# Gate projections in blocks of 128 features, half of them placed between the key and query tiles

## The chip, the cores and the metric

The kernel runs on one core of one Trainium2 chip. The time is device microseconds of one execution; the figure before the change is the median of three executions, and one further execution was taken with the hardware profiler.

## What is computed

One layer of a backbone over 1024 latent tokens of width 1024 (and 256 context tokens). Each token is normed and modulated to `h`, and one matrix `w_in` projects it to all inputs of two branches:

```
z = modulate(x, p['norm1_w'], sh1, sc1) @ w_in
q, k = z[..., 0:1024], z[..., 1024:2048]        # each rms_norm over 64, then rotary
v, u = z[..., 2048:3072], z[..., 3072:3584]
g = z[..., 3584:]                               # 2048 gate features
...
y_attn = diff_head_out(blocked_latent_diff_attention(q, k_all, v_all, lam), ...)
y_s5, _ = s5_branch(u, uc, p, update_ctx)       # linear recurrence, both directions, then GELU and GLU
g_s, g_a = split(g + b_gate, 2)
x = x + ga1 * ((sigmoid(g_s) * y_s5 + sigmoid(g_a) * y_attn) @ w_out)
x = x + ga2 * conv_ffn(modulate(x, p['norm2_w'], sh2, sc2), ...)
```

The gates `g` depend on `h` and on their weights alone. They are read much later, when the branches are merged.

## The kernel before

The modulated tokens stay in SBUF as two tables, `hTh` and `hTl` (a rounded high part and a remainder), and every projection is three products for each of the eight slices of the inner dimension: high by high, high by low and low by high. A unit of 128 outputs by 512 is thus 24 matmuls of 512 columns.

`phase_a` (L318) makes the projections in this order: u; keys (slabs 0 and 1, ten token tiles each, the last two of them context); values (slabs 2 and 3, ten tiles each); queries (slabs 5 and 6, eight tiles each); gates (slabs 7 to 10, L544). A slab is 512 features. `load_slab` (L586) fetches it in four quarters of 512 KB on the SP queue; ScalarE casts each quarter to the high part (L594) and GpSimd subtracts for the low part (L595). There are three buffers for raw weights and five each for high and low parts. The projected tile lies in a PSUM buffer "z", of which there are five for all projections.

- **Keys and queries.** `qk_post` (L633) takes a tile of 128 tokens: ScalarE squares (L638), VectorE reduces (L640, L641), ScalarE takes a square root (L644), VectorE the reciprocal and a Newton step (L645 to L648) and the two rotary products (L652, L656), GpSimd adds and scales (L657, L663), ScalarE scales six of the eight heads of a key tile (L662), TensorE transposes (L667), ScalarE and VectorE take the result out of PSUM (L670, L671), and SP stores it.
- **Recurrence.** Its parameters (`s5_params`, L758, generator `params`) are computed piece by piece beside the key tiles, mostly on VectorE. Its inputs are made beside the value tiles. `s5_scan` (L925) runs 158 steps one after the other, four small VectorE instructions each (L934 to L937): ten steps after each of the last value tiles, six after each query tile, and the rest in one call before the gates.
- **adaLN.** `adas` is a generator of small matmuls with loads of their own (L299, L302), one piece after each query tile.
- **Gates.** Here the weights are the stationary operand. For each of 16 blocks of 128 features and each half of the tokens there is one unit: 24 matmuls (L554 to L556), a tanh on ScalarE into one of two "stage" buffers (L558), and a store issued on ScalarE's queue (L559).
- **After the recurrence.** `s5_out_quad` (L940), eight of them, one after every second gate unit, at high priority: copies of the states on VectorE (L955, L956), matmuls (L962, L964); after every second one `s5_transpose` (L1187) stores the result. Then `s5_tail` (L1269) as a generator, one piece after each later gate unit: load and GELU (L1278, L1279), split into parts on VectorE and GpSimd (L1257, L1258), eight GLU units with a tanh (L1288), then sixteen branch units of 12 matmuls that end in L1310. The last four of the sixteen run inside the attention.
- **Attention** (`phase_b`, L969) follows. Its pool takes the memory of the token tables, which the gates read. Then come the merge, the output projection and the feed-forward (`phase_c`, L1324).

The order on each engine is set by a scheduler when the kernel is built: it takes the instructions by their order in the program (earlier ones first, high priority ahead of all) as they become ready on its own model of time. On the chip each engine runs its list in that fixed order.

Of the kernel before, what the change touches and what calls it, by code (L numbers as in the profile page):

```python
# [10 lines left out]
F32R = mybir.dt.float32r  # L11
I32 = mybir.dt.int32
AF = mybir.ActivationFunctionType
OP = mybir.AluOpType
# [4 lines left out]
P = 128  # L19
D = 1024  # L20
KT = D // P
L = 1024
NT = L // P
# [14 lines left out]
QUADS = G // 4  # L38
# [18 lines left out]
def pack(x, c, ctx, c_ctx, ada_w, ada_b, norm1_w, w_in, b_gate, q_norm_w, k_norm_w,  # L57
# [6 lines left out]
    def put(name, a):  # L64
        A[name] = np.ascontiguousarray(a)
# [10 lines left out]
    def perm64(a):  # L76
# [3 lines left out]
    w = np.asarray(w_in)[0]  # L80
    wq, wk = perm64(w[:, :1024]), perm64(w[:, 1024:2048])
    slabs = [wk[:, :512], wk[:, 512:], w[:, 2048:2560], w[:, 2560:3072], w[:, 3072:3584],
             wq[:, :512], wq[:, 512:]] + [w[:, 3584 + 512 * j:4096 + 512 * j] for j in range(4)]
    put("win", np.stack([s.reshape(2, 4, P, 512).transpose(0, 2, 1, 3) for s in slabs]))
    put("rows", np.concatenate([perm64(np.asarray(q_norm_w)), perm64(np.asarray(k_norm_w)), np.asarray(lam_q1),
                                np.asarray(lam_k1), np.asarray(lam_q2), np.asarray(lam_k2)], 1))
# [22 lines left out]
    def wtiles(a):  # L109
        k, m = a.shape  # L110
        return a.reshape(k // P, P, m // P, P).transpose(2, 1, 0, 3)

    put("wglu", wtiles(np.asarray(glu_w)[0]))
    put("wbs", wtiles(np.asarray(w_branch_s5)[0]))
    put("wba", wtiles(np.asarray(w_branch_attn)[0]))
# [8 lines left out]
    n = (NT * np.arange(P)[:, None] + np.arange(NT)[None, :])  # L124
# [10 lines left out]
def r32(ap):  # L135
    return ap.bitcast(F32)


class Kern:
# [178 lines left out]
    def phase_a(self):  # L318
# [91 lines left out]
        def project(tt, W, pz=None, ks=range(KT)):  # L410
            pz = self.t(ps, [P, 512], "z", 5) if pz is None else pz
            A = (hTh, hTl) if tt < NT else (cTh, cTl)
            tok = slice(tt % NT * P, tt % NT * P + P)
            for k in ks:
                wh, wl = W[0][k // 2][:, k % 2], W[1][k // 2][:, k % 2]
                hh, hl = A[0][k][:, tok], A[1][k][:, tok]
                nc.tensor.matmul(pz, hh, wh, start=k == 0, stop=False)  # L417
                nc.tensor.matmul(pz, hh, wl, start=False, stop=False)  # L418
                nc.tensor.matmul(pz, hl, wh, start=False, stop=k == KT - 1)  # L419
            return pz  # L420

        W = ([], [])
# [81 lines left out]
                next(params, None)  # L504
        zp, zp_st = self.pool("pk")
        self.rope_tables(zp, "K")
        for s in (0, 1):
            W = self.load_slab(wp, s)
            for tt in range(NKT):
                self.qk_post(zp, ps, project(tt, W), "K", s, tt)  # L510
                if tt % 4 == 3:
                    next(params, None)
        zp_st.close()
# [19 lines left out]
        for s in (5, 6):  # L533
            W = self.load_slab(wp, s)
            for tt in range(NT):
                self.qk_post(zp, ps, project(tt, W), "Q", s - 5, tt)
                next(adas, None)
                self.s5_scan(xp, self.scan_at + 6)
        zp_st.close()
        self.s5_scan(xp, NCH + NCC)  # L540
        yp, yp_st = self.pool("s5y")
        nq = 0
        tail = None
        for s in range(7, 11):  # L544
            W = self.load_slab(wp, s)
            for mm in range(4):
                m = (s - 7) * 4 + mm
                for hf in range(2):
                    tok = slice(hf * 512, hf * 512 + 512)
                    pz = self.t(ps, [P, 512], "z", 5)  # L550
                    for k in range(KT):
                        wh = W[0][k // 2][:, k % 2, mm * P:mm * P + P]
                        wl = W[1][k // 2][:, k % 2, mm * P:mm * P + P]
                        nc.tensor.matmul(pz, wh, hTh[k][:, tok], start=k == 0, stop=False)  # L554
                        nc.tensor.matmul(pz, wh, hTl[k][:, tok], start=False, stop=False)
                        nc.tensor.matmul(pz, wl, hTh[k][:, tok], start=False, stop=k == KT - 1)  # L556
                    g = self.t(gp, [P, 512], "stage", 2)
                    nc.scalar.activation(g, pz, AF.Tanh, scale=0.5, bias=self.hbg[:, m:m + 1])  # L558
                    nc.scalar.dma_start(self.Gd[m][:, tok], g)  # L559
                    next(adas, None)  # L560
                    if hf and nq < QUADS:
                        if nq % 2 == 0:
                            Yq = self.t(yp, [P, NT, P], "Yq", 1)
                        with self.tc.high_priority():
                            self.s5_out_quad(yp, ps, nq, Yq, xp)
                            nq += 1
                            if nq % 2 == 0:
                                self.s5_transpose(yp, ps, Yq, nq // 2 - 1)
                        if nq == QUADS:
                            for _ in adas:  # L570
                                pass
                            ap_st.close()
                            yp_st.close()
                            xp_st.close()
                            tail = self.s5_tail(ps)
                    elif tail:
                        next(tail, None)
        gp_st.close()
        wp_st.close()
        hp_st.close()  # L580
# [1 line left out]
        self.attn_open()  # L582
        for _ in tail:
            pass

    def load_slab(self, wp, s, qs=(0, 1, 2, 3)):  # L586
        nc = self.nc
# [941 lines left out]
```

## Time and profile before

| | |
|---|---|
| median of three executions | 2129.47 us (2129.38 to 2130.86) |
| the profiled execution | 2130.76 us |
| its span, first to last instruction | 2129.0 us |
| TensorE busy, matmuls | 2049.0 us |
| VectorE busy | 1185.0 us |
| GpSimd busy | 815.3 us |
| ScalarE busy | 741.8 us |

A busy share is the mean over stages that are limited by different things, so it is to be read stage by stage: in which stretch TensorE has idle time, and which engine is full in that stretch. TensorE's granted clock is given as a share of 2.4 GHz; its lower level is half of that. A matmul's record lasts longer than the distance to the next one (matmuls are pipelined), so the work of TensorE is measured from start to start.

### The profile page before, as it was taken

Reading aid. Unit: us, or ns where it says so; the run is one execution under the profiler, and the core shown is the slowest. Engines: PE = TensorE matmul, PEld = TensorE weight load, DVE = VectorE, ACT = ScalarE, POOL = GpSimd, SP = SyncE. Lnnn points to the kernel's source line nnn. Section 1 sums busy time; section 2 is a strip of 40 time slices with the busy share of each in tenths; the row PEclk is TensorE's granted clock in tenths of the full one; section 3 lists DMA queues with packets and bytes.
Section 4 is the critical chain, followed back from the end, with each engine's and each line's share of the span. In section 5 each row is a group of like instructions: output and inputs, shape, how many; then the busy total and the mean of one; then the engine's idle time right before and its main releaser. Section 6 shows DMA issues by size and latency. Waiting matters only on the chain. (4 is left out here: it accounts for less than half of the span.)

```text
span 2129.0 us, 28497 instructions
## 1 busy us (share of the span) xinstructions
PE 2049.0 (96%) x10656; PEld 1684.4 (79%) x10656; DVE 1185.0 (56%) x2363; ACT 741.8 (35%) x1349; POOL 815.3 (38%) x923
## 2 busy tenths in 40 slices
PE   6988999998999999999999989999999999999998
PEld 4766778865677887999999878878888888888887
DVE  6998944899962224888888653443323323233233
ACT  4434424221223313788888611332112212112121
POOL 1467411243211630366666646433323323223221
PEclk9998999999999999999999999999999999999999
DMA  9345575345667237322321145111111111111102
GB/s 324 105 116 139 124 207 175 120 123 164 202 198 233 95 107 234 93 78 86 113 78 53 36 163 179 49 45 50 52 47 50 46 43 45 47 52 46 50 15 99
DMA packets 150506, 227.84 MB, mean 107 GB/s; under 512 B 27104, under 2 KB 85856, under 8 KB 150368
## 3 DMA queue, kind: packets, MB, share of 16 engines
q1 hardware_dynamic: 140288, 207.67, 32.2%
q10 hardware_dynamic: 10080, 18.35, 2.3%
q8 instruction: 84, 1.38, 0.3%
q14 instruction: 54, 0.44, 0.1%
HBM read 168.76 MB, written 57.21 MB: 106 GB/s over the span
## 5 line engine op out<-in xcount | busy, mean ns | idle before, releaser
L1266 PE MATMUL up<-act,whi 128*128 128x512 f32 x704 | 276.5, 393 | 2.3 <-POOL act L1419 2.1
L1265 PE MATMUL up<-act,whi 128*128 128x512 f32 x704 | 276.1, 392 | 0.0
L1267 PE MATMUL up<-act,wlo 128*128 128x512 f32 x704 | 275.0, 391 | 0.0
L1505 DVE SCALAR_TENSOR_TENSOR y<-up,small,y 128x896 f32<-128x896 f32 (+1 forms) x176 | 123.9, 746 | 237.7 <-ACT y L1500 235.9
L1253 POOL TENSOR_TENSOR wlo<-wraw,whi 128x1024 fp32r<-128x1024 f32 (+1 forms) x64 | 141.5, 2212 | 276.6 <-ACT whi L1252 240.7
L1240 DVE TENSOR_REDUCE mx<-sc 128x1 f32<-128x1280 f32 x128 | 190.7, 1491 | 53.7 <-PE sc L1239 52.8
L595 POOL TENSOR_TENSOR wlo<-wraw,whi 128x1024 fp32r<-128x1024 f32 x40 | 97.4, 2451 | 244.4 <-ACT whi L594 242.4
L417 PE MATMUL z<-whi,hTh 128*128 128x512 f32 x448 | 182.2, 411 | 3.6 <-ACT hTh L406 3.6
L418 PE MATMUL z<-wlo,hTh 128*128 128x512 f32 x448 | 181.0, 405 | 0.4 <-POOL wlo L595 0.3
L419 PE MATMUL z<-whi,hTl 128*128 128x512 f32 x448 | 180.0, 404 | 0.2 <-DVE hTl L408 0.2
L993 ACT ACTIVATE e<-sc,mx 128x1280 f32<-128x1280 f32 x128 | 171.7, 1342 | 10.5 <-DVE mx L1240 8.9
L1038 PE MATMUL ta<-V,at 128*128 128x128 f32 x1280 | 168.1, 275 | 0.7 <-ACT at L1027 0.7
L1482 DVE SCALAR_TENSOR_TENSOR x<-z,modT,x 128x512 f32<-128x512 f32 x72 | 53.6, 750 | 203.6 <-PE z L1267 203.6
L1252 ACT CAST whi<-wraw 128x1024 fp32r<-128x1024 f32 (+1 forms) x64 | 62.0, 969 | 294.3 <-PE up L1266 156.1
L1266 PEld LDWEIGHTS up<-act,whi 128*128 128x128 f32 x704 | 132.3, 188 | 32.2 <-POOL act L1419 3.4
L1038 PEld LDWEIGHTS ta<-V,at 128*128 128x128 f32 x1280 | 155.5, 191 | 1.0 <-ACT at L1027 0.9
L1265 PEld LDWEIGHTS up<-act,whi 128*128 128x128 f32 x704 | 132.2, 188 | 29.8 <-DVE act L1417 0.2
L1267 PEld LDWEIGHTS up<-act,wlo 128*128 128x128 f32 x704 | 132.2, 188 | 28.7
L1238 PE MATMUL sc<-K,q 128*128 128x512 f32 (+1 forms) x384 | 148.2, 386 | 2.2 <-ACT e L993 2.2
L1239 PE MATMUL sc<-K,q 128*128 128x512 f32 (+1 forms) x384 | 131.8, 357 | 0.0
L1253 POOL TENSOR_TENSOR wdlo<-wdraw,wdhi 128x512 fp32r<-128x512 f32 (+1 forms) x40 | 56.3, 1409 | 183.5 <-ACT wdhi L1252 183.3
L1266 PE MATMUL z<-gt,wdhi 128*128 128x512 f32 x320 | 124.6, 389 | 1.0 <-POOL gt L1258 1.0
(436 smaller groups left out, 4610.1 us busy)
## 6 DMA issues: line engine op xcount, KB each, us to landing
wraw<-in_win_dram SPq DMA_DIRECT2D x44, 512.0 KB
wraw<-in_wup_dram SPq DMA_DIRECT2D x44, 512.0 KB
araw<-in_ada_dram SPq DMA_DIRECT2D x32, 512.0 KB
q<-Qd SPq DMA_DIRECT2D x128, 128.0 KB
Kd<-st SPq DMA_DIRECT2D x80, 128.0 KB
K<-Kd SPq DMA_DIRECT2D x16, 640.0 KB
aw<-in_ada_dram SPq DMA_DIRECT2D x16, 512.0 KB
Qd<-st SPq DMA_DIRECT2D x32, 256.0 KB
```

Source lines behind the costliest of these rows:

```text
L417: nc.tensor.matmul(pz, hh, wh, start=k == 0, stop=False)
L418: nc.tensor.matmul(pz, hh, wl, start=False, stop=False)
L419: nc.tensor.matmul(pz, hl, wh, start=False, stop=k == KT - 1)
L993: nc.scalar.activation(em, S[i]["sc"][m][:, :LK], AF.Exp, bias=S[i]["mx"][:, m:m + 1], accum_out=S[i]["l1"] if m else S[i]["l0"])
L1038: nc.tensor.matmul(PO[p][:, j * P:j * P + P], AT[p, kt // 2][:, kt % 2, j * P:j * P + P], W[:, kt], start=kt == 0, stop=kt == NKT - 1)
L1238: nc.tensor.matmul(sc[:, a:b], Q[0][:, m, qs], K[m][:, a:b], start=True, stop=False)
L1239: nc.tensor.matmul(sc[:, a:b], Q[1][:, m, qs], K[m][:, a:b], start=False, stop=True)
L1240: nc.vector.tensor_reduce(S["mx"][:, m:m + 1], sc[:, :LK], axis=AX.X, op=OP.max, negate=True)
L1253: nc.gpsimd.tensor_tensor(l, raw, r32(h), op=OP.subtract)
L1265: mm(o, W[0][:, k], ah[k], start=k == 0, stop=False)
L1266: mm(o, W[0][:, k], al[k], start=False, stop=False)
L1267: mm(o, W[1][:, k], ah[k], start=False, stop=k == n - 1)
```

## The change

The gate weights are packed as 16 blocks of 1024 by 128 (`wg`) and not as four slabs of 512 features. A generator `gates` yields after each unit. Four units are drawn beside each key slab and four beside each query slab, so that 16 of the 32 units stand there; the other 16 follow the queries as before. In each query slab, four tiles now carry eight scan steps (four on either side of a gate unit) and the other four carry four steps, where every tile had six. Of the units after the queries each of the first eight is followed by a quad (before: every second unit), and each of the last eight by a piece of the tail.

```
-             wq[:, :512], wq[:, 512:]] + [w[:, 3584 + 512 * j:4096 + 512 * j] for j in range(4)]
+             wq[:, :512], wq[:, 512:]]
...
+    put("wg", wtiles(w[:, 3584:]))
...
+        gates = self.gates(wp, ps, hTh, hTl)
         for s in (0, 1):
             W = self.load_slab(wp, s)
             for tt in range(NKT):
                 self.qk_post(zp, ps, project(tt, W), "K", s, tt)
+                if tt in (1, 2, 5, 6):
+                    next(gates)
                 if tt % 4 == 3:
                     next(params, None)
...
                 self.qk_post(zp, ps, project(tt, W), "Q", s - 5, tt)
+                if tt in (1, 2, 4, 5):
+                    self.s5_scan(xp, self.scan_at + 4)
+                    next(gates)
                 next(adas, None)
-                self.s5_scan(xp, self.scan_at + 6)
+                self.s5_scan(xp, self.scan_at + 4)
...
-        for s in range(7, 11):
-            W = self.load_slab(wp, s)
-            for mm in range(4):
...
+        for _ in gates:
+            next(adas, None)
+            if nq < QUADS:
...
+                with self.tc.high_priority():
+                    self.s5_out_quad(yp, ps, nq, Yq, xp)
...
+            else:
+                next(tail, None)
...
+    def gates(self, wp, ps, hTh, hTl):
+        nc = self.nc
+        for m in range(16):
+            blk = lambda x: x.rearrange("p a b -> p (a b)").rearrange("p (k n) -> p k n", k=KT)
+            raw = self.t(wp, [P, 2, 512], "wraw", 3)
+            nc.sync.dma_start(blk(raw), self.I["wg"][m])
+            h = self.t(wp, [P, 2, 512], "whi", 5, F32R)
+            l = self.t(wp, [P, 2, 512], "wlo", 5, F32R)
+            nc.scalar.copy(h, raw)
+            nc.gpsimd.tensor_tensor(l, raw, r32(h), op=OP.subtract)
+            W = blk(h), blk(l)
+            for hf in range(2):
+                tok = slice(hf * 512, hf * 512 + 512)
+                pz = self.t(ps, [P, 512], "z", 5)
+                self.gemm(pz, W, [x[:, tok] for x in hTh], [x[:, tok] for x in hTl])
+                g = self.t(self.gp, [P, 512], "stage", 2)
+                nc.scalar.activation(g, pz, AF.Tanh, scale=0.5, bias=self.hbg[:, m:m + 1])
+                nc.scalar.dma_start(self.Gd[m][:, tok], g)
+                yield
```

## Rows read from the trace of the kernel before

**Rows 1.** The page's first part: busy us, share of the span, instructions.

```profile
PE 2049.0 (96%) x10656; PEld 1684.4 (79%) x10656; DVE 1185.0 (56%) x2363; ACT 741.8 (35%) x1349; POOL 815.3 (38%) x923
```

**Rows 2.** By stretch: length, busy PE PEld DVE ACT POOL, granted clock, DMA, GB/s.

```profile
117.00:281.00 164.00, 141.98 (x918) 109.33 (x917) 148.53 (x296) 68.42 (x205) 99.56 (x95) 0.92 0.53 138
281.00:421.00 140.00, 139.44 (x735) 116.48 (x735) 70.70 (x196) 47.57 (x114) 22.00 (x11) 0.99 0.51 158
421.00:609.00 188.00, 172.90 (x735) 117.59 (x734) 181.75 (x646) 39.24 (x70) 65.83 (x44) 0.96 0.56 169
609.00:821.00 212.00, 212.00 (x1040) 172.14 (x1039) 57.08 (x66) 49.75 (x72) 62.88 (x38) 1.00 0.49 161
821.00:2129.00 1308.00, 1288.65 (x6757) 1097.73 (x6755) 635.02 (x891) 487.80 (x809) 523.44 (x703) 1.00 0.23 72
```

**Rows 3.** Waits of PE in 117 to 281: total us, times, longest us.

```profile
PE ta L667 <- ACT t L662: 9.7, 6, 4.4
```

**Rows 4.** VectorE and GpSimd in order of time, 470 to 474: start, us, instruction.

```profile
470.65 2.42 DVE L935 TENSOR_TENSOR sc<-X,A8b 128x64 f32<-128x64 f32 x1
...
473.64 0.22 DVE L935 TENSOR_TENSOR sc<-X,A8b 128x64 f32<-128x64 f32 x1
...
470.61 2.38 POOL L595 TENSOR_TENSOR wlo<-wraw,whi 128x1024 fp32r<-128x1024 f32 x1
```

**Rows 5.** GpSimd groups by line, 117 to 281 and 421 to 609: busy, mean ns, idle.

```profile
L595 POOL TENSOR_TENSOR wlo<-wraw,whi 128x1024 fp32r<-128x1024 f32 x8 | 20.5, 2578 | 6.4 <-ACT whi L594 4.3 <-PE z L419 2.0
...
L595 POOL TENSOR_TENSOR wlo<-wraw,whi 128x1024 fp32r<-128x1024 f32 x12 | 28.5, 2384 | 39.3 <-ACT whi L594 39.3
```

**Rows 6.** TensorE in order of time: a gate unit's first matmul, and the one after its last.

```profile
768.99 0.39 PE L554 MATMUL z<-hTh,whi 128*128 128x512 f32 x1
...
774.47 0.39 PE L1265 MATMUL ta<-h5h,whi 128*128 128x512 f32 x1
```

**Rows 7.** ScalarE and its queue in order of time around the first gate's tanh.

```profile
550.98 0.21 ACT L644 ACTIVATE qt<-qv 128x8 f32<-128x8 f32 x1 [5.61 <-DVE qv L641]
551.10 0.57 ACT L670 CAST st<-tb 128x512 fp32r<-128x512 f32 x1
551.68 1.28 ACT L558 ACT_TABLE_LOAD   x1
552.98 0.69 ACT L558 ACTIVATE stage<-z,hbg 128x512 f32<-128x512 f32 x1
...
553.70 0.33 ACTq L559 DMA_DIRECT2D Gd<-stage  x1
```

**Rows 8.** Who waited for the square root of L644: us, times (36 tiles).

```profile
  DVE qr L645: 3.8, 5
```

**Rows 9.** L554 alone (eight matmuls in a unit) by stretch: length, PE busy (count).

```profile
421.00:609.00 188.00, 31.15 (x77) 14.74 (x77) 0.96 0.56 169
609.00:821.00 212.00, 71.22 (x180) 33.60 (x179) 1.00 0.49 161
...
719.00:753.00 34.00, 8.14 (x21) 3.94 (x21) 1.00 0.14 47
753.00:821.00 68.00, 21.27 (x55) 10.13 (x54) 1.00 0.47 153
```

**Rows 10.** After the scan: its last instruction, quads' transposes, loads, GELU splits.

```profile
608.65 0.23 DVE L937 TENSOR_TENSOR X<-X,sc 128x64 f32<-128x64 f32 x1
...
L1193 PE MATMUL tb<-ident,Yq x16: 272/272/273, 625.6 to 679.6; 128*128 128x128 f32 x16
...
680.77 0.41 SPq L1278 DMA_DIRECT2D y<-Yd  x1
...
716.17 2.40 POOL L1258 TENSOR_TENSOR h5l<-y,h5h 128x1024 fp32r<-128x1024 f32 x1 [5.30 <-DVE h5h L1257]
```

**Rows 11.** GLU tanh, branch units and the attention's first matmul: min/median/max ns, first to last.

```profile
L1288 ACT ACTIVATE gth<-ta,hglub x4: 682/684/691, 721.7 to 748.2; 128x512 f32<-128x512 f32 x4
...
L1310 DVE SCALAR_TENSOR_TENSOR gate<-gate,tb x8: 675/689/689, 756.2 to 838.6; 128x512 f32<-128x512 f32 x8
...
820.94 0.40 PE L1238 MATMUL sc<-K,q 128*128 128x512 f32 x1
```

More of the change, by code (lines that the diff above doesn't have):

```diff
@@ L543, in phase_a @@
         tail = None
-        for s in range(7, 11):
-            W = self.load_slab(wp, s)
-            for mm in range(4):
[L547 to L577, printed above, removed]
@@ new lines, in phase_a @@
+        for _ in gates:
+            next(adas, None)
+            if nq < QUADS:
+                if nq % 2 == 0:
+                    Yq = self.t(yp, [P, NT, P], "Yq", 1)
+                with self.tc.high_priority():
+                    self.s5_out_quad(yp, ps, nq, Yq, xp)
+                    nq += 1
+                    if nq % 2 == 0:
+                        self.s5_transpose(yp, ps, Yq, nq // 2 - 1)
+                if nq == QUADS:
+                    for _ in adas:
+                        pass
+                    ap_st.close()
+                    yp_st.close()
+                    xp_st.close()
+                    tail = self.s5_tail(ps)
+            else:
+                next(tail, None)
```

## The prediction

> **What bounds the kernel now.** I read the page's busy shares first: TensorE is busy 96% of the span and no other engine over 56% [rows 1]. That alone would say that moving matmuls about gains nothing. The table of stretches says where it is not so [rows 2]. In the key stretch (117 to 281) TensorE is busy 141.98 of 164.00 us at a granted clock of 0.92, while VectorE is busy 148.53. In the query stretch (421 to 609) it is 172.90 of 188.00 at 0.96, with VectorE at 181.75. In the three stretches after and between, TensorE is full (139.44 of 140, 212.00 of 212, 1288.65 of 1308). So VectorE bounds the key and query stretches and TensorE the rest. The waits of the key stretch fit: TensorE stands at the transposes, because the scaled tile comes late [rows 3].
>
> What is lost on TensorE there: 164.00 - 141.98 = 22.0 us idle and 0.08 x 164 = 13.1 us by the clock, 35.1 us in all among the keys; 15.1 us idle and 0.04 x 188 = 7.5 us, 22.6 us in all among the queries. Together 57.7 us, the most that this change can win back by filling.
>
> From 609 on there is a second bound. The scan's last instruction is at 608.65, and what hangs on it is a chain: quads and transposes to 679.6, load and GELU of four tiles one after the other until 718.6, GLU units with the last tanh at 748.2, branch units, attention at 820.94 [rows 10, 11]. TensorE is full there only because gate units stand between the links.
>
> **The change part by part.** *A gate unit* is 774.47 - 768.99 = 5.48 us of TensorE [rows 6], the same 24 matmuls in either packing. Eight units, 43.8 us, go to each of the two VectorE-bound stretches. The instructions of loads, casts and subtractions stay 16 each for all gates, of the same sizes; only their places change, and a block needs one load where a slab needed four. I cost that at nothing, since TensorE doesn't wait in the gate stage.
>
> *Among the keys* 43.8 us of work meet 35.1 us of lost time, so TensorE's need grows by 8.7 us. VectorE's need grows as well, because of GpSimd. A subtraction of L595 at 470.61 takes 2.38 us, and the VectorE instruction that starts beside it takes 2.42 us where the same instruction takes 0.22 at 473.64 [rows 4]: the two shut each other out. There are 8 such subtractions among the keys now, 12 among the queries [rows 5]; four more blocks among the keys cost VectorE 4 x 2.2 = 8.8 us, in a stretch where it was bound. Bounds: nothing, if they fall into its 15.5 idle us, and 8.8 + 8.7 if the two needs don't overlap. I take 9 us.
>
> *Tanh between square roots.* Before, ScalarE loads its table for the square root once and for the gates' tanh once: the load at 551.68 follows the cast at once, lasts 1.28, and the tanh starts at 552.98, so a switch costs 1.30 us [rows 7]. Now a tanh stands between the square roots of neighbouring tiles, up to 16 x 2 = 32 loads, 41 us of ScalarE, which is busy 68 of 164 and 39 of 188 us in these stretches [rows 2] and takes it, as far as nobody waits. VectorE waits for the root in the reciprocal: today 3.8 us in 5 of 36 tiles [rows 8], so mostly there is other work between. Of the 16 roots that come behind a tanh each can cost between 0 and 1.3 us: bounds 0 and 20.8. I take a third, 7 us, nearer to the row of waits. The Trainium skill's page "ScalarE: Activation LUTs", section "What ACT_TABLE_LOAD costs", gives a switch 1.28 us for the load and as much again for a drain, 2.66 us as an estimate; this trace shows 1.30 with no gap for a drain. By the page the whole of ScalarE's added time would be 85 us.
>
> *Among the queries* the scan has 8 x 8 + 8 x 4 = 96 steps where it had 16 x 6 = 96: no cost or gain, only another order. The gate blocks' subtractions take the place of those that the slabs already did there (12); as TensorE gets further ahead, about one more falls in: 2 us. Bounds 0 and 4 x 2.2 = 8.8.
>
> *Queues.* Each moved unit issues its store on ScalarE's queue, 0.33 us [rows 7]; 16 of them, 5.3 us, lie in ScalarE's idle time. The loads stand on SP among the stores of keys and queries; a load waits there for one of five weight buffers, of which a slab holds four, and behind it wait the tile stores. The fifth buffer comes free after a block's second unit, two or three tiles ahead of the next use, so I cost it at nothing; without that cover a load is late by up to the 4.4 us of the longest wait of [rows 3], per block.
>
> So the scan ends 9 + 7 + 2 = 18 us later.
>
> *After the scan.* Before, 180 / 8 = 22.5 units lay here, 77 / 8 = 9.6 in the query stretch [rows 9]. Now 8 lie among the keys, and among the queries 9.6 plus 22.6 / 5.48 = 4.1 in the filled time; 10.3 remain. TensorE's own work after the scan falls from 212 to 212 - 12.2 x 5.48 = 145 us. But the chain doesn't shrink as far. From 753 to 821 stood 55 / 8 = 6.9 gate units between the branch units [rows 9]; without them the twelve branch units take 12 x 2.74 = 32.8 us (half of 5.48 each), 35 us less than 68. From 719 to 753 there were 21 / 8 = 2.6 units, 14 us; the splits of the last GLU outputs remain, so I take 6 of the 14. The quads (71 us) and the GELU loop (38 us) wait on stores, loads and two PSUM buffers, hardly on TensorE: 0, with a bound of 14 us less. So the stretch takes 212 - 35 - 6 = 171 us (157 to 177), and TensorE, with 145 us of work, is idle in it for some 26 us. What is late next is this chain: a part of the winnings is given back there.
>
> *Sum.* 2130.76 + 18 - 41 = 2107.8 us on the profiled execution, which lies 1.3 us above the median: about 2107 us by the median.
>
> **The rivals.** *All gaps are filled.* If the quads follow each other faster once fewer gates stand between them, the stretch after the scan is bound by its 145 us of work, and if the tables cost nothing the scan ends 9 us later: -67 + 9 = -58, 2071 us. For it: TensorE is full at every moment after 609, so how fast the chain could go isn't seen. Against: the GELU loop of 38 us with TensorE in no link of it.
>
> *ScalarE's fixed order turns against the tiles (slower).* If each of 32 table loads lands on the way of a key or query tile, the scan ends 9 + 2 + 41 = 52 us later, and 52 - 41 = +11: 2140 us. The change loses as soon as the scan ends more than 41 us later. For it: the first gate's tanh at 552.98 stood behind a root that waited 5.61 us for VectorE [rows 7], so ScalarE's list does stop for the slower engine. Against: ScalarE is at 42% and 21% there. The page named above makes this rival worse: with its drain, 52 becomes 96 us and the time 2184.
>
> *The gates fill nothing.* A unit takes one of five PSUM buffers that the tiles wait for; if gates push key tiles back one for one, the scan ends 44 us later and the change doesn't do what it says: +3, 2132 us. Against: a gate's buffer is free again as soon as its tanh has run.
>
> **How the numbers follow.** Forecast 0.50, all filled 0.22, ScalarE 0.13, fills nothing 0.15. From the forecast's bounds (scan later by 0 to 38, the chain 35 to 55 shorter) come -55 to +3 around it. The range 2074 to 2136 leaves out about half of the first rival and half of the second. About 0.2% (4.3 us) is what a measurement of this kernel can tell from no change. Faster by more: 0.45 + 0.22 + 0.03 = 0.70; within: 0.03 of the forecast, 0.06 of the last rival, 0.01 of the second, 0.10; slower: 0.20.
>
> **What would show it.** Right: TensorE's idle time and its clock losses in the key and query stretches nearly gone, with VectorE still full; 20 to 35 table loads; the scan's last L937 some 18 us later; new TensorE idle time between the quads and the GLU; attention's first L1238 near 798; nothing changed after it beyond a few us. Wrong: a scan that ends over 41 us later; no idle time after the scan (then the first rival); VectorE waiting for ScalarE at L645 by more than 20 us.

## The result, and the profile after

The changed kernel takes 2142.34 us (median; 2139.35 to 2145.97), 1.0056 times the time before, interval 1.0044 to 1.0068: 12 to 13 us slower, where 22 us faster was forecast. Its profiled execution took 2145.97 us with a span of 2144.2.

The page's first part (busy us, share of the span, instructions) hardly differs from [rows 1]; ScalarE has 44 us and 32 instructions more: the table loads, 1.28 us each, are 41 us of it.

```profile
PE 2051.2 (96%) x10656; PEld 1687.0 (79%) x10656; DVE 1188.8 (55%) x2363; ACT 785.5 (37%) x1381; POOL 815.5 (38%) x923
```

The table of stretches of the changed kernel (columns as in [rows 2]), cut at the matching events: keys, values, queries up to the scan's last instruction, from there to the end of the 12th branch unit, the rest.

```profile
117.00:307.00 190.00, 175.58 (x1145) 141.18 (x1144) 152.10 (x304) 100.29 (x230) 106.09 (x96) 0.96 0.56 151
307.00:446.00 139.00, 138.36 (x690) 115.87 (x689) 65.14 (x184) 47.06 (x115) 22.99 (x13) 1.00 0.45 142
446.00:637.00 191.00, 171.20 (x730) 121.59 (x729) 184.90 (x644) 62.69 (x89) 68.61 (x46) 0.96 0.45 137
637.00:842.00 205.00, 186.43 (x878) 141.90 (x877) 60.09 (x74) 43.07 (x64) 52.30 (x34) 0.93 0.60 191
842.00:2144.00 1302.00, 1284.21 (x6733) 1094.28 (x6731) 633.41 (x888) 483.50 (x803) 521.99 (x702) 1.00 0.23 69
```

The reader sees three things beside [rows 2]. The keys are 26 us longer, and what TensorE loses there (idle time, and the clock's share of the stretch) went from 35.1 to 14.4 + 0.04 x 190 = 22.0 us: 13 us filled by 43.8 us of units. (43.8 less the growth of 26 would give 17.5; the clock column is rounded, and the trace lacks a few matmul records.) The queries are 3 us longer and lose 19.8 + 0.04 x 191 = 27.4 us where they lost 22.6: nothing filled. And behind the scan, where TensorE was full before, 18.6 + 0.07 x 205 = 33 us are lost; some 26 us of idle time were forecast there, in a stretch of 171 us.

The stretch behind the scan, by events, in us after the scan's last instruction (which ends at 608.9 before and 637.2 after). The GLU's and the branch units' events are taken at the end of the last tanh and of the 12th unit:

| | before | after | forecast |
|---|---|---|---|
| first quad's matmul on the state | 4.9 | 19.0 | unchanged |
| last transpose of the quads | 71.0 | 88.3 | unchanged |
| first GELU | 80.3 | 103.7 | unchanged |
| fourth GELU | 105.4 | 135.0 | unchanged |
| last GLU tanh | 140.0 | 161.1 | 6 earlier |
| 12th branch unit | 218.9 | 204.8 | 41 earlier |

Two of these events as lines, the first quad's matmul and the 12th branch unit, before (L964, L1310) and after (L977, L1323):

```profile
613.75 0.38 PE L964 MATMUL ta<-wo,sg 128*128 128x128 f32 x2
827.13 0.69 DVE L1310 SCALAR_TENSOR_TENSOR gate<-gate,ta 128x512 f32<-128x512 f32 x1 [1.93 <-DMA gate<-Gd]
...
656.17 0.39 PE L977 MATMUL ta<-wo,sg 128*128 128x128 f32 x2
841.30 0.69 DVE L1323 SCALAR_TENSOR_TENSOR gate<-gate,ta 128x512 f32<-128x512 f32 x1 [3.14 <-DMA gate<-Gd]
```

So from the last GLU tanh to the 12th branch unit 78.9 us became 43.7, the 35 us that were forecast; but up to that tanh the stretch grew by 21 us. Views of SP's queue and of ScalarE show where. First SP's queue (start, us for the issues, line; a group is issued back to back) around the scan's end:

```profile
637.28 1.21 SPq L688 DMA_DIRECT2D Qd<-st  x2
638.58 1.36 SPq L958 DMA_DIRECT2D wo<-Wod  x2
640.00 7.91 SPq L964 DMA_DIRECT2D toep<-Td  x8
647.95 0.93 SPq L971 DMA_DIRECT2D utq<-UTd  x2
```

The loads of the first two quads stand right behind the last query stores, and these now come when the scan ends. Before, the queries' last tile was finished at 567.0, 42 us ahead of the scan's end, and the same loads had been issued from 568.48 on:

```profile
568.48 0.93 SPq L945 DMA_DIRECT2D wo<-Wod  x2
```

By the program the quads' pool takes over the query pool's memory, so the loads can't be issued before the query tiles are through with it. Then the queue at the quads' end in the changed kernel:

```profile
706.46 0.96 SPq L971 DMA_DIRECT2D utq<-UTd  x2
707.52 22.13 SPq L300 DMA_DIRECT2D araw<-in_ada_dram  x6
729.74 0.41 SPq L1291 DMA_DIRECT2D y<-Yd  x1
```

The same place in the kernel before, where two such loads followed the last quads' and y came at 680.77:

```profile
662.12 1.32 SPq L958 DMA_DIRECT2D utq<-UTd  x2
663.86 1.41 SPq L299 DMA_DIRECT2D araw<-in_ada_dram  x2
```

Six of adaLN's 512 KB loads stand ahead of the first y load; with two buffers each waits for the one before last to be used, 22.13 us in all, and y, which before was issued 0.9 us after the quads' last transpose [rows 10], comes 4 us after it. The GELU isn't held by y, though, but by adaLN's end, through the order of ScalarE's list (start, us, in brackets the idle time before and what ended it):

```profile
737.31 0.59 ACT L307 COPY stage<-ada 128x512 f32<-128x512 f32 x1 [8.93 <-PE ada L303]
737.79 0.69 ACT L595 ACTIVATE stage<-z,hbg 128x512 f32<-128x512 f32 x1
...
738.89 0.69 ACT L595 ACTIVATE stage<-z,hbg 128x512 f32<-128x512 f32 x1 [0.40 <-PE ta L310]
739.60 1.28 ACT L1292 ACT_TABLE_LOAD   x1
```

ScalarE stands idle for 8.93 us until adaLN's last matmul is done (737.3), copies its result (L307), waits once more for adaLN's transposes (L310), and comes to the GELU at 740.90 with no wait of its own. The loop that draws the gates explains the number of steps that are left so late: before, a quad stood at every second gate unit and an adaLN step at every unit, so 16 steps lay among the quads; now a quad stands at every unit, 8 steps lie there, and 10 of the 34 are drained behind them. Last, the GELU loop on ScalarE in the changed kernel:

```profile
740.90 1.06 ACT L1292 ACTIVATE y<-y 128x1024 f32<-128x1024 f32 x1
752.74 1.06 ACT L1292 ACTIVATE y<-y 128x1024 f32<-128x1024 f32 x1 [0.46 <-ACT stage L595]
761.24 1.06 ACT L1292 ACTIVATE y<-y 128x1024 f32<-128x1024 f32 x1 [3.44 <-DMA y<-Yd]
772.20 1.06 ACT L1292 ACTIVATE y<-y 128x1024 f32<-128x1024 f32 x1 [9.90 <-DMA y<-Yd]
```

And SP's queue beside it:

```profile
757.45 0.86 SPq L1227 DMA_DIRECT2D K<-Kd  x2
758.40 0.44 SPq L1230 DMA_DIRECT2D V<-Vd  x1
758.93 2.62 SPq L1240 DMA_DIRECT2D q<-Qd  x1
...
763.59 0.61 SPq L1240 DMA_DIRECT2D q<-Qd  x1
765.48 0.33 SPq L1291 DMA_DIRECT2D y<-Yd  x1
```

The first loads of the attention now stand ahead of the fourth y load, since fewer gate units are left; ScalarE waits 9.90 us for that y, and 4.91 before. They don't hold its issue: y has one buffer, which the third tile's subtraction on GpSimd left at 765.45, and the load was issued at 765.48. But it took 6.7 us from there to the GELU, where the fourth load before took 3.4:

```profile
710.90 0.32 SPq L1278 DMA_DIRECT2D y<-Yd  x1
714.30 1.06 ACT L1279 ACTIVATE y<-y 128x1024 f32<-128x1024 f32 x1 [4.91 <-DMA y<-Yd]
```

That the attention's transfers slow it down fits, but no run isolates it. This is half of the 6 us by which the loop grew; the other half is the second GELU, which stands behind a gate's tanh.

### The profile page after: what moved, and what is told of

The parts are those of the page before. It is cut to its first block, busy times and chain, and to the rows that moved or that the text cites. A ratio compares the mean times of both kernels' runs of the same rounds, so it can differ in the third digit from the quotient of the medians.

```text
span 2144.2 us, 28518 instructions
## 1 busy us (share of the span) xinstructions
PE 2051.2 (96%) x10656; PEld 1687.0 (79%) x10656; DVE 1188.8 (55%) x2363; ACT 785.5 (37%) x1381; POOL 815.5 (38%) x923
## 5 line engine op out<-in xcount | busy, mean ns | idle before, releaser
L1280 PE MATMUL z<-gt,wdlo 128*128 128x512 f32 x320 | 124.3, 389 | 0.0
```

Of the source, the lines that this page charges most:

```text
L1280: mm(o, W[1][:, k], ah[k], start=False, stop=k == n - 1)
```

## The experiments

Times are medians, ratios to the kernel before, which was run beside each. "The keys end" is the subtraction of the last key tile (L684 in the changed kernel), at 286.2 us before and 312.5 after. Each such place is read from one trace; the end of the first key tile alone lies between 126.0 and 129.7 us in these traces, with little altered ahead of it, so a difference of 1 or 2 us between two runs can be chance.

```profile
285.55 0.68 DVE L671 TENSOR_TENSOR st<-ta,st 128x512 fp32r<-128x512 f32 x1
...
311.78 0.69 DVE L684 TENSOR_TENSOR st<-ta,st 128x512 fp32r<-128x512 f32 x1 [3.12 <-ACT st L683]
```

### Which part of the change costs what

Packing alone (no unit moved, a quad at every second gate as before), the packing with the units among the keys, and with those among the queries:

```diff
  blocks_only, queries_only
-                if tt in (1, 2, 5, 6):
-                    next(gates)
  blocks_only, keys_only
-                if tt in (1, 2, 4, 5):
-                    self.s5_scan(xp, self.scan_at + 4)
-                    next(gates)
                 next(adas, None)
-                self.s5_scan(xp, self.scan_at + 4)
+                self.s5_scan(xp, self.scan_at + 6)
  blocks_only
-        for _ in gates:
+        for i, _ in enumerate(gates):
             next(adas, None)
+            if nq < QUADS and i % 2 == 0:
+                continue
```

> The gate weights come as 16 blocks and the units by the generator, but none is moved: all 32 units after the queries, a quad after every second unit, six scan steps after each query tile, as before. All theories of the loss put it on the moving, so this should be as before: 2129 us, within 4 us. If the packing itself costs something (a strided stationary operand, later loads), it shows here alone.

> Eight units stand among the keys as in the change; the query stage is as before (six steps per tile, no gates between tiles). Theory A (the gates ahead of query tiles let the queries end with the scan, at 638 and not 42 us ahead of it, and so the quads' loads start only then): here the queries end well ahead of the scan again, the first quad follows the scan's end by about 5 us, the scan ends about 26 us later than before, and the stretch after it is some 35 to 40 us shorter than 212: about 2117 us, faster than before. Rival B (the late quads have another cause, the shorter filler after the scan): the first quad is 19 us late here too and the time stays at 2135 to 2143 us.

> No unit among the keys; eight among the queries with the scan steps of the change. Theory A: the scan ends only about 3 us later than before, the queries end with it, the first quad is about 19 us behind the scan's end and not 5, and 22 or so gate units fill that gap: 2120 to 2132 us, and keys_only and this one do not add up to the change. If the loss of the change came from the keys alone, this one would be 2110 to 2118 us.

| | us | ratio (interval) | keys end | queries' last tile | scan ends | 12th branch unit |
|---|---|---|---|---|---|---|
| before | 2129.43 | | 286.2 | 567.0 | 608.9 | 827.8 |
| blocks_only | 2139.13 | 1.0041 (1.0026 to 1.0056) | 286.1 | 571.0 | 611.1 | 836.6 |
| keys_only | 2128.59 | 0.9987 (0.9977 to 0.9998) | 312.7 | 594.6 | 634.7 | 825.8 |
| queries_only | 2138.53 | 1.0042 (1.0025 to 1.0059) | 284.9 | 612.5 | 611.6 | 834.3 |
| changed | 2142.34 | 1.0056 (1.0044 to 1.0068) | 312.5 | 638.1 | 637.2 | 842.0 |

The units among the keys cost 26 us there in both kernels that have them. Those among the queries delay the queries' last tile from 42 us ahead of the scan's end to the scan's end itself, and leave the scan where it was. The units among the keys alone give a kernel as fast as before. Measured from blocks_only, which has the same packing, they win 10.5 us, those among the queries 0.6, and both together lose 3.2: the two moves don't add up. Both single moves came out slower than their theories A (about 2117, and 2120 to 2132 us), which had reckoned the packing at nothing. And the packing costs 9 us by itself. It is lost among the queries (columns as in [rows 2]):

```profile
421.00:611.00 190.00, 168.79 (x718) 114.95 (x717) 183.77 (x647) 38.95 (x70) 67.72 (x47) 0.95 0.55 167
```

That is 21.2 + 0.05 x 190 = 30.7 us of TensorE where 22.6 were lost before, and behind the scan TensorE is full in both, so the 8 us aren't made up. TensorE's waits of blocks_only in 386 to 611 us (total us, times, longest) begin with one that the kernel before doesn't have (keys_only has it too, 10.8 us).

```profile
PE tb L310 <- DVE X L947: 10.6, 1, 10.6
```

L310 is adaLN's first group of transposes; in another list order it stands behind a PSUM buffer that VectorE, busy with the scan, frees late. To test it, one adaLN step was drawn ahead of the query loop, so that the group completes inside it:

```diff
+        next(adas)
         for s in (5, 6):
             W = self.load_slab(wp, s)
```

> blocks_only (the new packing alone, no unit moved, 2139.1 us) with one adaLN step drawn ahead of the query loop, so that the first adaLN group is complete inside it. In blocks_only TensorE stood 10.6 us at that group's transposes behind one of the scan's instructions, and 3.95 us at that place in the kernel before. Theory J (the packing costs 9 us only by that wait, a place in TensorE's list): the wait falls under 5 us and the time to 2129 to 2134. Rival K (the packing itself costs TensorE time behind the scan): 2137 to 2141.

2137.32 us (1.0026, 1.0015 to 1.0038). The wait went from 10.6 to 7.1 us and other waits took up some of the rest, so this run neither clears nor convicts it: the time lies in the range of rival K, but theory J's condition, a wait under 5 us, wasn't met. That the packing costs some 6 to 9 us is shown; that it is this wait is argued only.

### The keys: what doesn't explain 26 us

Tables: the tanh of the 16 units among keys and queries replaced by Identity, so that no table is switched (the tanh is left out, and with it their values). GpSimd: in keys_only the four blocks' subtractions left out (the high part stands for the low one):

```diff
  no_table
+                f = AF.Identity if m < 8 else AF.Tanh
-                nc.scalar.activation(g, pz, AF.Tanh, scale=0.5, bias=self.hbg[:, m:m + 1])
+                nc.scalar.activation(g, pz, f, scale=0.5, bias=self.hbg[:, m:m + 1])
  keys_nosub
-            nc.gpsimd.tensor_tensor(l, raw, r32(h), op=OP.subtract)
+            if m >= 4:
+                nc.gpsimd.tensor_tensor(l, raw, r32(h), op=OP.subtract)
-            W = blk(h), blk(l)
+            W = blk(h), blk(l if m >= 4 else h)
```

> The change, with the tanh of the 16 moved units replaced by Identity of the same size (their gates are left without tanh), so that ScalarE's table isn't switched among key and query tiles: 6 table loads and not 38, nothing else altered. Theory C (the 26 us by which the keys end later come from ScalarE's 16 switches there, 21 us of a list that VectorE waits for): the keys end 10 to 15 us earlier than in the change, and the time falls to 2124 to 2132 us. Rival D (they come from the four more subtractions on GpSimd and from TensorE's 44 us of work meeting 35 us of room): the keys end where they do in the change and the time stays at 2138 to 2143 us.

> Eight units among the keys, none among the queries, and the GpSimd subtraction of the four key blocks is left out (the low part of the weights is taken to be the high part, so eight units' values differ). Theory C (the blocks' four GpSimd subtractions shut VectorE out, about 2.2 us each as the prediction put it, and are what the keys pay beyond the units' own TensorE time): the keys' last tile ends 7 to 10 us earlier, at 303 to 306 us in place of 312.7. Rival D (the keys pay because TensorE's and ScalarE's work stands in one fixed order with the key tiles'): it ends within 2 us of 312.7.

no_table took 2140.20 us (1.0051, 1.0036 to 1.0066), 6 table loads in place of 38, and the keys ended at 310.5: the 16 loads that stand among the keys, 20.5 us of ScalarE, cost some 2 us there, and all 32 brought the scan's end forward by 2.6 when they were left out. The trace of the changed kernel shows why so little: 15 of the 17 table loads for the square root are followed by a further wait of 0.15 to 6.7 us for the root's input, so they ended before anything could have used them. keys_nosub took 2127.45 us (0.9987, 0.9976 to 0.9998) and the keys ended at 311.2, 1.5 us earlier. The stretch of the keys in keys_only, and in keys_nosub:

```profile
117.00:308.00 191.00, 176.76 (x1150) 142.00 (x1149) 153.34 (x304) 100.21 (x230) 106.72 (x97) 0.96 0.56 151
```

```profile
117.00:306.50 189.50, 175.16 (x1150) 139.75 (x1148) 142.44 (x306) 100.50 (x231) 99.18 (x93) 0.98 0.56 153
```

VectorE's busy time (the third figure) fell by 10.9 us, where the exclusion of [rows 4] gives 8.8 for four subtractions, and the stretch by only 1.5. With units among the keys VectorE is busy 153 of 191 us: it no longer bounds them.

### The keys: how many units, how large, what of them

```diff
  keys_4
-                if tt in (1, 2, 5, 6):
+                if tt in (1, 5):
  keys_half: as keys_only, and
-                if tt in (1, 2, 5, 6):
+                if tt in (0, 1, 2, 3, 4, 5, 6, 7):
                     next(gates)
...
+                self.gemm(pz, W, *xs, 0, 4)
+                if m < 4:
+                    yield
+                self.gemm(pz, W, *xs, 4, 8)
  keys_quarter: four parts of two k, and
-                self.qk_post(zp, ps, project(tt, W), "K", s, tt)
+                z = project(tt, W)
+                next(gates)
+                self.qk_post(zp, ps, z, "K", s, tt)
+                if tt < 6:
+                    next(gates)
  keys_short
+                n = 2 if m < 4 else KT
+                self.gemm(pz, W, [x[:, tok] for x in hTh[:n]], [x[:, tok] for x in hTl[:n]])
  keys_t1x3
-        t1 = self.t(zp, [P, 8, HD], "t1", 2)
+        t1 = self.t(zp, [P, 8, HD], "t1", 3 if kind == "K" else 2)
```

> Four units among the keys in place of eight (after tiles 1 and 5 of each slab), none among the queries. With eight the keys' last tile came 26.3 us later, 3.3 us a unit against 5.48 us of TensorE work in one. Theory E (each unit costs the same, a fixed 3.3 us): 299 to 300 us, 13 us later than without units. Rival F (the gaps take in the first units for little, and the later ones at full price): 290 to 294 us, and a time 3 to 6 us below that with eight units, 2122 to 2126.

> The same eight units among the keys as in keys_only, none among the queries, but each unit cut into two halves of 12 matmuls, which stand at 16 of the 20 key tiles in place of 8. The keys' lost 50 us of TensorE were some 2.5 us in each of 20 tiles. Theory G (a unit fills only the gap of the tile at which it stands, and what it is longer than that gap it adds; the gaps of the other tiles stay): a half of 2.74 us fits one gap nearly, the keys' last tile ends at 289 to 297 us in place of 312.7, and the time is 2108 to 2117. Rival H (a unit costs 3.3 us by the work it brings to the other engines, however it is cut): 309 to 313 us, and 2125 to 2130.

> As keys_half, but each of the eight units among the keys in four parts of 6 matmuls, one between a tile's projection and its transposes at every tile and one behind the transposes at 12 of 20. Theory G in the form that the halves left it (what TensorE still loses among the keys, 21 us with whole units and 14.5 with halves by idle time and clock, is the waits at the transposes where no gate matmul stands): another 3 to 7 us, the keys' last tile at 299 to 304 us, the loss at 7 to 12 us, time 2118 to 2123. Rival I (the rest isn't a matter of where the units stand): 305 to 308 us, 2124 to 2127.

> keys_only with the eight units among the keys cut to 6 of their 24 matmuls (their values are left wrong), everything else of them kept: block loads, casts, subtractions, PSUM buffers, tanh, stores. That takes 8 x 4.1 = 33 us of matmuls out of a stretch that is 26.4 us longer than without units. Theory M (it is the units' TensorE time that lengthens the keys, since little of it falls into gaps): the keys' last tile ends at 284 to 292 us. Rival N (it is what a unit brings to the other engines and their lists): 300 to 312 us.

> keys_only with three buffers in place of two for the tile that VectorE writes and TensorE's transposes read (t1), for the keys alone. Theory L (a unit ahead of a tile's transposes holds t1, so VectorE, which stands idle 37.7 us there in place of 15.5, can't run ahead): the keys' last tile ends at 303 to 309 us, VectorE's idle time falls under 32 us, and the time is 2119 to 2125. Rival O (the buffers aren't what holds VectorE): 311 to 314 us and 2125 to 2130.

| | us | ratio (interval) | keys end | later than before |
|---|---|---|---|---|
| keys_4 | 2130.74 | 0.9994 (0.9983 to 1.0004) | 298.4 | 12.2 |
| keys_only (8 units) | 2128.59 | 0.9987 (0.9977 to 0.9998) | 312.7 | 26.5 |
| keys_half | 2125.52 | 0.9973 (0.9962 to 0.9984) | 306.5 | 20.3 |
| keys_quarter | 2132.39 | 1.0006 (0.9996 to 1.0016) | 315.2 | 29.0 |
| keys_short | 2119.81 | 0.9945 (0.9931 to 0.9960) | 300.3 | 14.1 |
| keys_t1x3 | 2126.35 | 0.9979 (0.9968 to 0.9990) | 311.6 | 25.4 |

Four units cost 3.05 us each and eight 3.3: the cost is in proportion, the gaps don't take in the first ones for less. Halves won 6.2 us, which ends the keys between the ranges of theories G and H; quarters lost them again, so the theory that a unit fills just the gap of its own tile, with 2.5 us a tile, falls in the form that the finer cut is the better one. (The quarters also stand at another place, partly ahead of the transposes, so that run changes two things; and the 2.5 us a tile, 50 in all, were too much: by idle time and clock keys_only loses 14.2 + 0.04 x 191 = 22 us there, 1.1 a tile.) A third t1 buffer did nothing (VectorE idle 38.1 us against 37.7). keys_short says most: with 6 of 24 matmuls in a unit the keys end 12.4 us earlier. The 33 us of matmuls that were left out had thus cost 12.4, 0.38 us for one of TensorE; and units that are nearly empty, 11 us of matmuls, still cost 14.1. By the same rate those 11 us account for 4, and some 10 us hang on what else a unit brings, of which tables and subtractions are some 3.5. What stays lost is seen in TensorE's waits among the keys of the changed kernel (compare [rows 3]):

```profile
PE tb L680 <- ACT t L675: 8.3, 4, 5.0
PE ta L680 <- ACT t L675: 5.0, 2, 4.2
```

The transposes wait for the scaled tile as before, in other tiles, since the units stand elsewhere in TensorE's list; 13.3 us of the 14.4 idle us are these. In keys_half they are 7.2, beside 3.2 for a cast of weights. Which instructions of a nearly empty unit hold the tiles up stays open.

### Behind the scan: two chains end together

Quad 0's loads get buffers of their own and are issued with the first query slab; the adaLN steps are drawn once more behind each unit among the queries; and both together:

```diff
  early_quads
         self.rope_tables(zp, "Q")
+        ep, ep_st = self.pool("s5e", "right")
...
             W = self.load_slab(wp, s)
+            if s == 5:
+                self.early = self.s5_out_load(ep, 0)
...
+        wo, tq, ut = self.s5_out_load(self.pools[q % 2], q) if q else self.early
  early_ada
                     next(gates)
+                    next(adas, None)
  keys_early: early_quads without the units among the queries
  early_both: early_quads and early_ada
```

> The changed kernel with one thing moved: quad 0's three loads (wo, toep, utq) get buffers of their own, opened beside the query pool, and are issued right after the first query slab's load; the later quads take the two buffer sets in turn. Theory A (the quads stand late because their loads wait for the query pool's memory and stand on SP behind the last query stores): the first quad matmul starts 4 to 8 us after the scan's end in place of 19.0, the 14 gate units still left then fill later gaps of TensorE (735 to 775 us) instead, and the time falls by 8 to 14 us, to 2128 to 2134. Rival B (TensorE has other work then anyway, or adaLN's last matmuls at 737 us and the memory they hold set the GELU's start): the first quad comes earlier but the GELU still starts near 740 and the time stays at 2140 to 2143.

> The changed kernel with one thing moved: adaLN's steps (a 512 KB load and four matmuls each) are drawn one more time behind each of the eight units among the queries, so 24 of the 34 stand among the queries in place of 16, and two in place of ten are left when the quads are done. Theory A (the ten steps that the change leaves behind the quads, and the memory they hold, set the GELU's start): adaLN's last matmul falls from 737 to 705 to 722 us, the GELU starts at 728 to 735 in place of 740.9, and the time falls by 5 to 12 us, to 2130 to 2137. Rival B (the late first quad sets it): the GELU starts within 2 us of 740 and the time is 2139 to 2143.

> The changed kernel with early_quads' early loads and early_ada's earlier adaLN steps together. With the early loads alone the quads' transposes ended at 713.9 us in place of 725.5, yet the GELU began at 739.9 and the time did not move. Theory A (two chains end there, quads and adaLN, and each alone hides the other): the GELU starts at 722 to 729 us, the time is 2124 to 2132. Rival B (what follows is bound by other things, the loads of attention's first head or the gates' loads): the GELU starts earlier but the time stays within 4 us of 2142.

> Eight units among the keys, none among the queries, and quad 0's loads issued early as in early_quads. With units only among the keys the first quad came 11.1 us after the scan, and TensorE lost 11.5 us at 780 to 820 us, after the gates had run out. Theory A: first quad 4 to 8 us after the scan's end, the later stretch is filled, time 2118 to 2125, below the kernel before. Rival B: TensorE was never idle between the scan's end and the first quad there, so the time stays at 2127 to 2130.

| | us | ratio (interval) | scan ends | first quad | last transpose | adaLN's last matmul | first GELU | 12th branch unit |
|---|---|---|---|---|---|---|---|---|
| changed | 2142.34 | 1.0056 (1.0044 to 1.0068) | 637.2 | 656.2 | 725.5 | 737.3 | 740.9 | 842.0 |
| early_quads | 2142.70 | 1.0055 (1.0036 to 1.0074) | 636.8 | 647.3 | 713.9 | 736.3 | 739.9 | 838.9 |
| early_ada | 2130.16 | 0.9998 (0.9988 to 1.0007) | 635.4 | 654.1 | 720.3 | 683.4 | 728.8 | 826.1 |
| early_both | 2121.55 | 0.9957 (0.9940 to 0.9973) | 638.4 | 651.5 | 717.4 | 697.1 | 725.5 | 818.2 |
| keys_early | 2127.05 | 0.9983 (0.9971 to 0.9996) | 632.9 | 642.7 | 703.4 | 685.8 | 715.0 | 825.1 |

The early loads alone brought the quads 9 to 12 us forward and won nothing. SP's queue in early_quads shows eight adaLN loads that now take 29.42 us, with y issued 2 us sooner than in the changed kernel, and ScalarE's list shows what holds the GELU: as in the changed kernel it comes to it only after adaLN's last matmul, for which it stands idle 19.26 us.

```profile
698.08 29.42 SPq L300 DMA_DIRECT2D araw<-in_ada_dram  x8
727.59 0.38 SPq L1301 DMA_DIRECT2D y<-Yd  x1
...
736.37 0.59 ACT L307 COPY stage<-ada 128x512 f32<-128x512 f32 x1 [19.26 <-PE ada L303]
```

In the changed kernel, early_quads, queries_only and no_table alike the first GELU starts 3.6 us after adaLN's last matmul. In early_ada that matmul is at 683.4, y is issued 0.1 us after the quads' last transpose, and the GELU starts 8.5 us after that transpose (9.3 in the kernel before).

adaLN's steps drawn earlier won 12 us by themselves, and with them out of the way the early loads another 9. In early_both nothing stands ahead of the y loads, all four go out before the attention's:

```profile
700.12 0.80 SPq L970 DMA_DIRECT2D utq<-UTd  x2
717.50 0.32 SPq L1302 DMA_DIRECT2D y<-Yd  x1
...
730.85 0.32 SPq L1302 DMA_DIRECT2D y<-Yd  x1
...
738.59 8.13 SPq L1302 DMA_DIRECT2D y<-Yd  x2
747.40 2.85 SPq L1238 DMA_DIRECT2D K<-Kd  x2
```

The GELU loop is back to 24.7 us from its first to its fourth start (31.3 in the changed kernel, 25.2 before), and the stretch behind the scan is as follows.

```profile
638.00:818.00 180.00, 171.76 (x839) 137.43 (x840) 60.41 (x74) 42.63 (x63) 50.91 (x34) 0.97 0.59 189
```

From the scan's end to the 12th branch unit 179.8 us, where 204.8 were measured and 178 forecast (219 less 41). That the sums meet is in part luck: the fourth GELU stands 111.8 us behind the scan's end where 105.4 was forecast, and the GLU and branch units make up 4.5 us more than forecast. keys_early is no faster than keys_only: there the queries end 40 us ahead of the scan, adaLN ends before the quads do, and TensorE was busy 70.36 of the 71 us from 609 to 680 in keys_only, so an early load wins nothing. In early_both the first quad still comes 13 us behind the scan, not 5; TensorE's units stand ahead of it. What that costs wasn't tried.

The two findings together, the halves among the keys and early_both:

> The changed kernel with quad 0's early loads, the earlier adaLN steps, and the eight units among the keys cut into halves at 16 tiles. Theory: the winnings stand in different stretches and add up: 2121.5 (early loads and adaLN) less the 6.2 us by which the halves ended the keys earlier gives 2113 to 2118, below both kernels. Rival: what the keys win is given back behind the scan, where TensorE's filler is gone: 2119 to 2123.

2120.29 us (0.9947, 0.9935 to 0.9959). Of the runs whose results are whole it is the fastest, but not by more than early_both's interval. The keys end at 310.8, 2.4 us before early_both's where the halves had won 6.2; counted from the end of the first key tile, which came at 129.5 here and at 128.2 in early_both, it is 3.8 against 5.5. So most of the halves' gain is there at the keys' end, and only 1.3 us of it in the time; where the rest goes wasn't looked for.

## Why the prediction was wrong

The bound was read rightly: what the keys and queries add reaches the scan's end, and what follows the attention's start doesn't change (1301 us before and 1302 after the 12th branch unit). The sum failed by 38 us on the profiled execution (2145.97 against 2107.8): 10 at the scan's end, 27 behind it, 1 after. None of its three signs of being wrong appeared (the scan ended 28 us later and not over 41, TensorE has idle time behind the scan, VectorE waited 2.1 us for the root and not over 20): they watched its own terms, and the largest part was lost in a term that was put at nothing. One slip in its sums: the upper bounds of its three terms are 17.5, 20.8 and 8.8 us, 47 in all, and not 38; with 47 its forecast would have reached some 2141 us.

- **"43.8 us of work meet 35.1 us of lost time" (+9 us among the keys): wrong.** It was +26. Lost time was taken for one pool that a unit may draw on wherever it stands. It is a sum of waits at the transposes (13.3 of the 14.4 us of idle time that are left) and of time at the low clock, and the units stand at other places of TensorE's list: 13 of the 35 us were filled. The term for the GpSimd subtractions, 8.8 us, measured 1.5. So the same 9 us were built from the wrong parts: the subtractions hardly cost, and what TensorE keeps losing costs most. Of the 26 us, 14 stay with units that are nearly empty (keys_short), and what in them holds the tiles up stays open.
- **Tables (7 us of 0 to 20.8): oversized.** The number, 32 loads, was right; without them the keys end 2 us earlier and the scan (634.6) 2.6 us. The Trainium skill, "ScalarE: Activation LUTs", section "What ACT_TABLE_LOAD costs", rates a switch at about twice the load's 1.28 us, for a drain beside it. The traces don't show that: a switch took 1.30 us in [rows 7], and the measurement decides. Of 32 x 1.28 = 41 us, 2 to 3 reached the end, in stretches where ScalarE is idle 47% (keys) and 67% (queries). The rival in which ScalarE's order delays the scan by 52 us named about the right time, 2140 us, by a mechanism that didn't occur: the scan ended 28 us later.
- **Queries (+2 us): right for the scan** (225 us long before, 228 after), **wrong in what it leaves behind.** Forecast were 13.7 units there and 10.3 behind the scan; counted by their matmuls, as in the prediction, there were 10.5, where 9.4 had been, and 13.5 behind it. TensorE's lost time there wasn't filled at all.
- **Packing (nothing): wrong,** 9 us by itself, though the counts of instructions were right. The paragraph on the queues also lets a load wait for one of five weight buffers; loads go into the raw buffers, of which there are three.
- **"The quads and the GELU loop ... 0": the step that failed most.** They began 14 us later in relation to the scan, then lost another 3 in the quads, 6 ahead of the first GELU and 6 in its loop, 30 in all. That the quads need TensorE little was true; what they need is loads, and these were taken as given where they stood: behind the last query stores, in the query pool's memory, with 42 us to spare that the moved units used up. Of the 14 us early_quads gives 8.5 to the loads (first quad 10.5 us behind the scan); what the other 5.6 hang on wasn't tried. I also passed over the adaLN steps that the gate loop draws. Halving their number per quad was in the diff, and the GELU then stood behind the last of them.
- **Branch units (-35 us): right,** 78.9 to 43.7. GLU, -6 forecast: -8.5 (34.6 to 26.1 us from the fourth GELU to the last tanh).

That the chain behind the scan could have been had is shown by early_both: 179.8 us against 178. What is left between the forecast and early_both's profiled execution (2121.63) is the scan's end, 638.4 where 608.9 + 18 was forecast, 11.5 us, and 2 us behind it: the chain as a whole was sized rightly, its links less so, and what was missed is two things that stand in its way, the quads' late loads and adaLN's late steps.

## What to carry to other kernels

Time that an engine loses in a stretch is not a pool: here a little over a third of it was filled, and how the units were cut and where they stood in the engine's fixed list changed that (halves won 6 us, quarters that stood elsewhere lost them again). When a step moves a stage's end, list what sits behind that stage on the load queue and in its memory, and count every generator that the edited loop draws, whatever it belongs to; a chain with slack of 42 us is off the path only until the move has used the slack. And where two chains end at one place, freeing the one that ends first shows nothing (early_quads, 0 us), though it is worth 9 us once the other is freed: free both before calling either innocent.

## What the runs showed of the hardware

- Loads on SP's queue were issued in the order of its list. Six adaLN loads that each waited for one of two buffers took 22.13 us there, eight took 29.42, and the y load behind them was issued 4 and 14 us after the quads' last transpose, where before, in early_ada and in early_both it was issued 0.1 to 0.9 us after it.
- ScalarE kept its list's order too: it stood idle 8.93 and 19.26 us at adaLN's copy, with the GELU behind it.
- VectorE's 10.9 us that went with GpSimd's four subtractions, and the 20.5 us of table loads on ScalarE among the keys, moved the end of the keys by 1.5 and 2 us only. Busy time that an exclusion or a switch added to an engine that waited anyway was nearly free here.
